# Attention scores on one core: two batches interleaved in 8 KB loads, all loads ahead of the stores, and head pairs in block-diagonal q weights

## Chip, cores and metric

The kernel runs on one core of a Trainium2 chip. The metric is the device time of one execution in microseconds (us), as the median of several runs.

## What is computed

For each of 8 batches and 8 heads, the scores of 512 queries against 512 keys of 64 elements, scaled by 1/8. Inputs and output are float32 in DRAM.

```python
batch, heads, seq, dim = 8, 8, 512, 64
# q, k: (batch, heads, seq, dim) float32
scale = 1.0 / np.sqrt(q.shape[-1])
return (np.einsum('bhqd,bhkd->bhqk', q, k) * scale).astype(np.float32)
```

The inputs are 16.8 MB together, the output is 67.1 MB.

## The kernel before

The kernel goes through the batches one by one. For each batch `load` (L56, L57) brings k and q in one transfer of 1 MB each into `kf` and `qf`. The eight heads are cut in two halves x of four heads g. A partition holds, for one head g and one stretch m of R = 16 adjacent sequence rows, the rows of both halves: two runs of 16 x 64 floats, 4 KB each. On the DRAM side the transfer is 128 entries of (g m) with two runs each, on the SBUF side 128 partitions.

The loads are issued on the queue of SyncE (SP), four batches ahead: those of batches 0 to 3 at the start, each further one after the first pair of stores of an earlier batch.

Each batch is cast to bf16 (L87) into `kb` and `qb`, where the two halves x stand side by side in 128 columns. GpSimd (POOL) does it for all batches but the first, which VectorE (DVE) and ScalarE (ACT) share. TensorE (PE) then transposes 128 x 128 blocks of k (L95) and q (L103) through an identity matrix into PSUM tiles `tp` of 128 x 1024. VectorE copies those of k into `kT` (L97), ScalarE those of q into `qT` (L105). After the transposes the 64 elements of half x = 0 are in partitions 0 to 63, those of x = 1 in 64 to 127.

The scores of a head need only 64 of the 128 rows of TensorE, so each matmul (L119) uses a quarter of the array: 64 rows (the half x) by 64 columns (64 queries, one of two heads h). Four such matmuls with 512 keys each fill one half w of two PSUM tiles `ps`:

```python
nc.tensor.matmul(out=pss[x][h * U:(h + 1) * U, w, :],
                 lhsT=qTh[rows, i + w, g, :], rhs=kTh[rows, g, :],
                 start=True, stop=True, tile_position=(x * D, h * U))
```

`evacuate` scales a `ps` tile (128 x 1024 floats) into the output tile `o`, in turn on ScalarE (L71) and VectorE (L73). An `o` tile is 2 MB: 128 partitions with 8 query rows of 512 scores each, 16 KB that lie together in DRAM. Each is stored in one transfer on SP's queue (L128), so there are 32 stores. There are six `o` buffers, and raw, bf16 and transposed buffers for 4, 2 and 2 batches.

A scheduler orders the instructions of each engine by the priorities of the program's order and by free buffers; each engine then executes its own list in order, and SP's list holds loads and stores together.

Of the kernel before, what the change touches and what calls it, by code (L numbers as in the profile page):

```python
# [1 line left out]

# [5 lines left out]


@with_exitstack  # L10
def kernel(
    ctx: ExitStack,
    tc: tile.TileContext,
    q: bass.AP,
    k: bass.AP,
    out: bass.AP,
):

    nc = tc.nc
    B, H, S, D = q.shape
    scale = 1.0 / (D ** 0.5)
    P = 128
    G = H // 2
    M = P // G
    R = S // M
    RO = 8  # L30
    HP = RO * P // S
    U = P // HP
    JJ = R // RO

    f32 = mybir.dt.float32
    bf16 = mybir.dt.bfloat16

    q_r = q.rearrange("b (x g) (m j) d -> b (g m) x (j d)", x=2, j=R)
    k_r = k.rearrange("b (x g) (m j) d -> b (g m) x (j d)", x=2, j=R)
    out_r = out.rearrange("b (x n h) (u i) k -> b x n (h u) i k", x=2, h=HP, i=RO)  # L40

    consts = ctx.enter_context(tc.tile_pool(name="consts", bufs=1))
    raw_pool = ctx.enter_context(tc.tile_pool(name="raw", bufs=4))
    bf_pool = ctx.enter_context(tc.tile_pool(name="bf", bufs=2))
    t_pool = ctx.enter_context(tc.tile_pool(name="t", bufs=2))
    out_pool = ctx.enter_context(tc.tile_pool(name="out", bufs=6))
    tpsum_pool = ctx.enter_context(tc.tile_pool(name="tpsum", bufs=2, space=bass.MemoryType.PSUM))
    psum_pool = ctx.enter_context(tc.tile_pool(name="psum", bufs=3, space=bass.MemoryType.PSUM))

    AHEAD = 4  # L50
    raws = {}

    def load(b):
        kf = raw_pool.tile([P, 2, R * D], f32, name="kf")
        qf = raw_pool.tile([P, 2, R * D], f32, name="qf")
        nc.sync.dma_start(out=kf, in_=k_r[b])  # L56
        nc.sync.dma_start(out=qf, in_=q_r[b])  # L57
        raws[b] = (qf, kf)

    load(0)  # L60
    identity = consts.tile([P, P], dtype=bf16)
    make_identity(nc, identity)
    for b in range(1, AHEAD):
        load(b)

    n_evac = 0

    def evacuate(dst, src):
        nonlocal n_evac
        if n_evac % 2 == 0:  # L70
            nc.scalar.mul(out=dst, in_=src, mul=scale)  # L71
        else:
            nc.vector.tensor_scalar(out=dst, in0=src, scalar1=scale, scalar2=None,  # L73
                                    op0=mybir.AluOpType.mult)
        n_evac += 1

    for b in range(B):
        qf, kf = raws.pop(b)
        kb = bf_pool.tile([P, R, 2, D], bf16, name="kb")
        qb = bf_pool.tile([P, R, 2, D], bf16, name="qb")  # L80
        for slab, dst in ((kf, kb), (qf, qb)):
            for x in range(2):
                if b > 0:
                    copy = nc.gpsimd.tensor_copy
                else:
                    copy = (nc.vector.tensor_copy, nc.scalar.copy)[x]
                copy(out=dst[:, :, x, :], in_=slab[:, x].rearrange("p (j d) -> p j d", j=R))  # L87


        kT = t_pool.tile([P, P, R], bf16, name="kT")  # L90
        qT = t_pool.tile([P, RO, P, JJ], bf16, name="qT")
        for j0 in range(0, R, 8):
            tp = tpsum_pool.tile([P, 8, P], bf16, name="tp")
            for j in range(8):
                nc.tensor.transpose(out=tp[:, j, :], identity=identity,  # L95
                                    in_=kb[:, j0 + j].rearrange("p x d -> p (x d)"))
            nc.vector.tensor_copy(out=kT[:, :, j0:j0 + 8], in_=tp.rearrange("d j p -> d p j"))  # L97
        IW = 8 // JJ
        for i0 in range(0, RO, IW):
            tp = tpsum_pool.tile([P, IW, JJ, P], bf16, name="tp")  # L100
            for i in range(IW):
                for jj in range(JJ):
                    nc.tensor.transpose(out=tp[:, i, jj, :], identity=identity,  # L103
                                        in_=qb[:, RO * jj + i0 + i].rearrange("p x d -> p (x d)"))
            nc.scalar.copy(out=qT[:, i0:i0 + IW], in_=tp.rearrange("d i jj p -> d i p jj"))  # L105

        kTh = kT.rearrange("d (g m) j -> d g (m j)", g=G)
        qTh = qT.rearrange("d i (g m) jj -> d i g (m jj)", g=G)
        for g0 in range(0, G, 2):
            os = [out_pool.tile([P, 2 // HP, RO, S], f32, name="o") for _ in range(2)]  # L110
            for n in range(2 // HP):
                for i in range(0, RO, 2):
                    pss = [psum_pool.tile([P, 2, S], f32, name="ps") for _ in range(2)]
                    for w in range(2):
                        for h in range(HP):
                            g = g0 + n * HP + h
                            for x in range(2):
                                rows = slice(x * D, (x + 1) * D)
                                nc.tensor.matmul(out=pss[x][h * U:(h + 1) * U, w, :],  # L119
                                                 lhsT=qTh[rows, i + w, g, :],  # L120
                                                 rhs=kTh[rows, g, :],
                                                 start=True, stop=True,
                                                 tile_position=(x * D, h * U))
                    for x in range(2):
                        evacuate(os[x][:, n, i:i + 2, :], pss[x])
            for x in range(2):
                n0 = g0 // HP
                nc.sync.dma_start(  # L128
                    out=out_r[b, x, n0:n0 + 2 // HP].rearrange("n p i k -> p n (i k)"),
                    in_=os[x].rearrange("p n i k -> p n (i k)"))  # L130
            if g0 == 0 and b + AHEAD < B:
                load(b + AHEAD)


# [1 line left out]
_INS = ['q', 'k']  # L136
_OUTS = [((8, 8, 512, 512), 'float32')]


# [23 lines left out]
```

## Time and profile before

| What | Value |
|---|---|
| Median of 9 runs | 205.96 us (205.76 to 206.25) |
| The profiled execution | 205.96 us, span 204.0 us |
| PE busy | 130.2 us (64% of the span) |
| DVE busy | 94.5 us (46%) |
| ACT busy | 82.9 us (41%) |
| POOL busy | 29.0 us (14%) |
| DMA | 84.01 MB, 8,969 packets, mean 412 GB/s |

The span goes from the first to the last instruction that the profile shows; the execution's own time has about 2 us around it. Busy times are sums over the span, and the engines run side by side. A DMA transfer is cut into packets that sixteen DMA engines move; its time to landing counts from its issue on SP's queue to the last of its bytes.

### The profile page before, as it was taken

What the parts mean: (1) busy time and instruction counts of PE and PEld (TensorE: products, weight loads), DVE (VectorE), ACT (ScalarE), POOL (GpSimd) and SP (SyncE); (2) the same over time, 40 slices, a digit from 0 to 9 for tenths busy, and PEclk for the clock granted to TensorE, in tenths of its full rate; (3) what the DMA queues carried; (4) which work ended last, traced back from release to release, by engine and by line L of the source; (5) the groups of instructions that cost most, each with busy time, mean ns of one, the idle gap of its engine ahead of it and who ended that gap; (6) DMA issues with size and microseconds to landing.
All of it is one profiled execution on the core that took longest, in us unless ns stands there. A gap on an engine that the chain in (4) does not pass through costs nothing.

```text
span 204.0 us, 1911 instructions
## 1 busy us (share of the span) xinstructions
PE 130.2 (64%) x768; PEld 45.0 (22%) x768; DVE 94.5 (46%) x82; ACT 82.9 (41%) x83; POOL 29.0 (14%) x34
## 2 busy tenths in 40 slices
PE   0398878775969659696486955969777677600000
PEld 0363423261103511034110421104211111000000
DVE  0549896912639036490546706366718081800000
ACT  2476978263522625227252453417552515200000
POOL 1077530510006100070000700000000000000000
PEclk9999999855555555558555585555555555555555
DMA  6999999999999999999999999999999999999991
GB/s 206 421 410 411 445 418 402 446 430 421 437 402 433 440 424 417 434 425 434 437 404 426 435 418 440 434 421 437 421 430 443 422 430 424 434 437 418 440 408 58
DMA packets 8969, 84.01 MB, mean 412 GB/s; under 512 B 768, under 2 KB 768, under 8 KB 4864
## 3 DMA queue, kind: packets, MB, share of 16 engines
q1 hardware_dynamic: 8960, 83.89, 97.6%
q8 instruction: 6, 0.10, 0.2%
q14 instruction: 3, 0.02, 0.0%
HBM read 16.78 MB, written 67.11 MB: 411 GB/s over the span
## 4 chain that ended last, share of the span: by engine, by line
DMA 60%; DVE 16%; PE 6%; ACT 4%; issue 1%; SPq 0%; DVEq 0%
DMA out_dram<-o 57%; DVE o L73 12%; PE ps L119 4%; DMA qf<-in_q_dram 3%; DVE kT L97 3%; ACT o L71 2%; ACT qT L105 1%; PE tp L103 1%; PE tp L95 1%; DVE qb L87 0%; SPq L56 0%; SPq L128 0%; DVEq L73 0%
## 5 line engine op out<-in xcount | busy, mean ns | idle before, releaser
L119 PE MATMUL ps<-kT,qT 64*64 64x512 bf16 x512 | 103.6, 559 | 37.5 <-ACT o L71 23.9
L73 DVE TENSOR_SCALAR o<-ps 128x1024 f32<-128x1024 f32 x64 | 75.2, 1219 | 76.3 <-DMA out_dram<-o 65.0
L71 ACT ACTIVATE o<-ps 128x1024 f32<-128x1024 f32 x64 | 64.5, 1025 | 77.1 <-PE ps L119 65.9
L119 PEld LDWEIGHTS <-qT 64*64 64x64 bf16 x512 | 22.5, 124 | 110.6 <-issue 107.9
L87 POOL CAST kb<-kf 128x1024 bf16<-128x1024 f32 x14 | 14.2, 1040 | 81.0 <-DMA kf<-in_k_dram 80.5
L105 ACT COPY qT<-tp 128x1024 bf16<-128x1024 bf16 x16 | 16.2, 1014 | 12.7 <-PE tp L103 12.4
L97 DVE COPY kT<-tp 128x1024 bf16<-128x1024 bf16 x16 | 18.9, 1216 | 0.6 <-PE tp L95 0.6
L95 PE MATMUL tp<-identity,kb 128*128 128x128 bf16 x128 | 13.2, 267 | 7.7 <-ACT kb L87 6.8
L103 PE MATMUL tp<-identity,qb 128*128 128x128 bf16 x128 | 15.1, 286 | 2.2 <-DVE kT L97 1.4
L87 POOL CAST qb<-qf 128x1024 bf16<-128x1024 f32 x14 | 14.2, 1040 | 6.1 <-DMA qf<-in_q_dram 4.2
L103 PEld LDWEIGHTS <-qb 128*128 128x128 bf16 x128 | 11.7, 131 | 9.6 <-issue 8.6
L95 PEld LDWEIGHTS <-kb 128*128 128x128 bf16 x128 | 11.0, 123 | 11.4 <-ACT kb L87 6.8
L87 DVE CAST kb<-kf 128x1024 bf16<-128x1024 f32 x1 | 0.7, 695 | 5.7 <-DMA kf<-in_k_dram 5.7
L87 ACT CAST kb<-kf 128x1024 bf16<-128x1024 f32 x1 | 1.0, 1045 | 3.6 <-DMA kf<-in_k_dram 3.6
L87 ACT CAST qb<-qf 128x1024 bf16<-128x1024 f32 x1 | 1.0, 1044 | 1.5 <-DMA qf<-in_q_dram 1.5
L87 ACT ACT_TABLE_LOAD x1 | 1.3, 1283 | 0.7 <-PEq L147 0.7
L87 DVE CAST qb<-qf 128x1024 bf16<-128x1024 f32 x1 | 0.7, 695 | 1.8 <-DMA qf<-in_q_dram 1.8
masks.py:199 POOL TENSOR_SCALAR_AFFINE_SELECT identity<-identity 128x128 bf16<-128x128 bf16 x1 | 0.3, 292 | 0.1
masks.py:197 POOL MEMSET identity<- 128x128 bf16 x1 | 0.2, 204 | 0.3 <-POOLq L147 0.3
L147 POOL MEMSET const-float32-0.0<- 128x1 f32 x1 | 0.1, 98 | 0.2 <-issue 0.2
L147 POOL MEMSET const-bfloat16-1.0<- 128x1 bf16 x1 | 0.1, 102 | 0.0
L147 POOL MEMSET const-uint8-127<- 128x1 uint8 x1 | 0.1, 102 | 0.0
(1 smaller groups left out, 0.1 us busy)
## 6 DMA issues: line engine op xcount, KB each, us to landing
out_dram<-o SPq DMA_DIRECT2D x32, 2048.0 KB, 25.0
kf<-in_k_dram SPq DMA_DIRECT2D x8, 1024.0 KB, 17.0
qf<-in_q_dram SPq DMA_DIRECT2D x8, 1024.0 KB, 19.5
```

The costliest lines, as they stand in the source:

```text
L71: nc.scalar.mul(out=dst, in_=src, mul=scale)
L73: nc.vector.tensor_scalar(out=dst, in0=src, scalar1=scale, scalar2=None, op0=mybir.AluOpType.mult)
L87: copy(out=dst[:, :, x, :], in_=slab[:, x].rearrange("p (j d) -> p j d", j=R))
L95: nc.tensor.transpose(out=tp[:, j, :], identity=identity, in_=kb[:, j0 + j].rearrange("p x d -> p (x d)"))
L97: nc.vector.tensor_copy(out=kT[:, :, j0:j0 + 8], in_=tp.rearrange("d j p -> d p j"))
L103: nc.tensor.transpose(out=tp[:, i, jj, :], identity=identity, in_=qb[:, RO * jj + i0 + i].rearrange("p x d -> p (x d)"))
L105: nc.scalar.copy(out=qT[:, i0:i0 + IW], in_=tp.rearrange("d i jj p -> d i p jj"))
L119: nc.tensor.matmul(out=pss[x][h * U:(h + 1) * U, w, :], lhsT=qTh[rows, i + w, g, :], rhs=kTh[rows, g, :], start=True, stop=True, tile_posi ...
L147: nc = _bacc.Bacc("TRN2", target_bir_lowering=False, num_devices=1)
```

## The change

There are two parts.

The first is another layout of the work. A unit is now two batches (v, with b = 0 or 1), so there are four units. A head number is n and x, with x the lower bit, so the two heads of a pair are adjacent. A transfer brings one x of one unit: 128 partitions of (m, b, n), m being a stretch of R = 32 sequence rows, 8 KB in one run. On the DRAM side this is 16 entries of m with 8 runs (b n) each; on the SBUF side it is 128 partitions. There are 16 loads of 1 MB as before. `load_and_cast` is called for all units before any scores, so that on SP's queue the 16 loads stand ahead of all 32 stores; four raw buffers, now of 8 KB for each partition, hold the loads in flight, and a load waits until the load four before it is cast. The casts, of 128 x 2048 elements each, go into five `xb` buffers. There are five `o` buffers instead of six.

The second is the use of TensorE. The transposed q of the two heads x of a pair goes into a tile `qz` whose other quarters are zero: rows of x = 0 have their 64 queries in columns 0 to 63, rows of x = 1 in columns 64 to 127. One matmul over the full array (128 rows, 128 columns, 512 keys) gives the scores of both heads; two such matmuls do what four in quarters did. Two `qz` tiles are cleared once at the start, one quarter by VectorE and three by GpSimd. The copies of transposed k are shared between VectorE and ScalarE, and a transposed q tile takes two copies of 64 partitions each, one on either engine.

In the changed kernel the loads are L70, the casts L75, the clears L82, the transposes L91 (k) and L100 (q), the copies L94 and L105, the matmul L116, the evacuations L57 and L59, the stores L120.

```diff
-    G = H // 2
-    M = P // G
+    UNITS = B // 2
+    C = H
+    M = P // C
     R = S // M
     RO = 8
-    HP = RO * P // S
-    U = P // HP
+    U = S // RO
     JJ = R // RO
...
-    q_r = q.rearrange("b (x g) (m j) d -> b (g m) x (j d)", x=2, j=R)
-    k_r = k.rearrange("b (x g) (m j) d -> b (g m) x (j d)", x=2, j=R)
-    out_r = out.rearrange("b (x n h) (u i) k -> b x n (h u) i k", x=2, h=HP, i=RO)
+    q_r = q.rearrange("(v b) (n x) (m j) d -> v x m (b n) (j d)", b=2, x=2, j=R)
+    k_r = k.rearrange("(v b) (n x) (m j) d -> v x m (b n) (j d)", b=2, x=2, j=R)
+    out_r = out.rearrange("(v b) (n x) (u i) k -> v (b n) (x u) (i k)", b=2, x=2, i=RO)
...
-    bf_pool = ctx.enter_context(tc.tile_pool(name="bf", bufs=2))
+    bf_pool = ctx.enter_context(tc.tile_pool(name="bf", bufs=5))
...
-    out_pool = ctx.enter_context(tc.tile_pool(name="out", bufs=6))
+    out_pool = ctx.enter_context(tc.tile_pool(name="out", bufs=5))
...
+    def load_and_cast(v):
+        both = []
+        for src in (k_r, q_r):
+            xb = bf_pool.tile([P, R, 2, D], bf16, name="xb")
             for x in range(2):
-                if b > 0:
+                xf = raw_pool.tile([P, R * D], f32, name="xf")
+                nc.sync.dma_start(out=xf, in_=src[v, x])
+                if v > 0:
                     copy = nc.gpsimd.tensor_copy
                 else:
                     copy = (nc.vector.tensor_copy, nc.scalar.copy)[x]
-                copy(out=dst[:, :, x, :], in_=slab[:, x].rearrange("p (j d) -> p j d", j=R))
+                copy(out=xb[:, :, x, :], in_=xf.rearrange("p (j d) -> p j d", j=R))
+            both.append(xb)
+        return both
+    def clear(engine, qz, x):
+        rows = slice(x * D, (x + 1) * D)
+        engine.memset(qz[rows, :, :, (1 - x) * U:(2 - x) * U], 0.0)
...
+            copy = (nc.vector.tensor_copy, nc.scalar.copy)[n % 2]
+            copy(out=kT[:, :, :, j0:j0 + 8].rearrange("d c m j -> d m c j"),
+                 in_=tp.rearrange("d j (m c) -> d m c j", c=C))
...
-            nc.scalar.copy(out=qT[:, i0:i0 + IW], in_=tp.rearrange("d i jj p -> d i p jj"))
+            for x in range(2):
+                rows = slice(x * D, (x + 1) * D)
+                copy = (nc.vector.tensor_copy, nc.scalar.copy)[x]
+                copy(out=qz[rows, i0:i0 + IW, :, x * U:(x + 1) * U]
+                     .rearrange("d i c (m jj) -> d i c m jj", jj=JJ),
+                     in_=tp[rows].rearrange("d i jj (m c) -> d i c m jj", c=C))
+        return kT, qz
...
+    def scores(v, c, kT, qz):
+        o = out_pool.tile([P, RO, S], f32, name="o")
+        for i in range(0, RO, 2):
+            ps = psum_pool.tile([P, 2, S], f32, name="ps")
+            for w in range(2):
+                nc.tensor.matmul(out=ps[:, w, :], lhsT=qz[:, i + w, c, :],
+                                 rhs=kT[:, c].rearrange("d m j -> d (m j)"),
+                                 start=True, stop=True)
+            evacuate(o[:, i:i + 2, :], ps)
+        nc.sync.dma_start(out=out_r[v, c], in_=o.rearrange("p i k -> p (i k)"))
+
+    cast = [load_and_cast(0)]
...
+    qzs = [consts.tile([P, RO, C, P], bf16, name=f"qz{n}") for n in range(2)]
+    clear(nc.vector, qzs[0], 0)
+    clear(nc.gpsimd, qzs[0], 1)
+    for x in range(2):
+        clear(nc.gpsimd, qzs[1], x)
+    for v in range(1, UNITS):
+        cast.append(load_and_cast(v))
+
+    ts = {0: transpose(0, *cast[0])}
+    for v in range(UNITS):
+        for c in range(C):
+            scores(v, c, *ts[v])
+            if c == C // 2 - 1 and v + 1 < UNITS:
+                ts[v + 1] = transpose(v + 1, *cast[v + 1])
```

More of the change, by code (lines that the diff above doesn't have):

```diff
@@ L26 @@
     P = 128
-    G = H // 2
-    M = P // G
+    UNITS = B // 2
+    C = H
+    M = P // C
     R = S // M
     RO = 8
-    HP = RO * P // S
-    U = P // HP
+    U = S // RO
     JJ = R // RO
+    IW = 8 // JJ
     f32 = mybir.dt.float32
     bf16 = mybir.dt.bfloat16
-    q_r = q.rearrange("b (x g) (m j) d -> b (g m) x (j d)", x=2, j=R)
-    k_r = k.rearrange("b (x g) (m j) d -> b (g m) x (j d)", x=2, j=R)
-    out_r = out.rearrange("b (x n h) (u i) k -> b x n (h u) i k", x=2, h=HP, i=RO)
+    q_r = q.rearrange("(v b) (n x) (m j) d -> v x m (b n) (j d)", b=2, x=2, j=R)
+    k_r = k.rearrange("(v b) (n x) (m j) d -> v x m (b n) (j d)", b=2, x=2, j=R)
+    out_r = out.rearrange("(v b) (n x) (u i) k -> v (b n) (x u) (i k)", b=2, x=2, i=RO)
     consts = ctx.enter_context(tc.tile_pool(name="consts", bufs=1))
     raw_pool = ctx.enter_context(tc.tile_pool(name="raw", bufs=4))
-    bf_pool = ctx.enter_context(tc.tile_pool(name="bf", bufs=2))
+    bf_pool = ctx.enter_context(tc.tile_pool(name="bf", bufs=5))
     t_pool = ctx.enter_context(tc.tile_pool(name="t", bufs=2))
-    out_pool = ctx.enter_context(tc.tile_pool(name="out", bufs=6))
+    out_pool = ctx.enter_context(tc.tile_pool(name="out", bufs=5))
     tpsum_pool = ctx.enter_context(tc.tile_pool(name="tpsum", bufs=2, space=bass.MemoryType.PSUM))
     psum_pool = ctx.enter_context(tc.tile_pool(name="psum", bufs=3, space=bass.MemoryType.PSUM))
[L50 to L64, printed above, removed]
     n_evac = 0
@@ L75, in evacuate @@
         n_evac += 1
[L77 to L81, printed above, removed]
+    def load_and_cast(v):
+        both = []
+        for src in (k_r, q_r):
+            xb = bf_pool.tile([P, R, 2, D], bf16, name="xb")
             for x in range(2):
-                if b > 0:
+                xf = raw_pool.tile([P, R * D], f32, name="xf")
+                nc.sync.dma_start(out=xf, in_=src[v, x])
+                if v > 0:
                     copy = nc.gpsimd.tensor_copy
@@ L86, with transpose @@
                     copy = (nc.vector.tensor_copy, nc.scalar.copy)[x]
[L87 to L92, printed above, removed]
+                copy(out=xb[:, :, x, :], in_=xf.rearrange("p (j d) -> p j d", j=R))
[4 more added lines that the diff above has]
+        engine.memset(qz[rows, :, :, (1 - x) * U:(2 - x) * U], 0.0)
+    def transpose(v, kb, qb):
+        kT = t_pool.tile([P, C, M, R], bf16, name="kT")
+        qz = qzs[v % 2]
+        for n, j0 in enumerate(range(0, R, 8)):
             tp = tpsum_pool.tile([P, 8, P], bf16, name="tp")
@@ L96 @@
                                     in_=kb[:, j0 + j].rearrange("p x d -> p (x d)"))
-            nc.vector.tensor_copy(out=kT[:, :, j0:j0 + 8], in_=tp.rearrange("d j p -> d p j"))
-        IW = 8 // JJ
+            copy = (nc.vector.tensor_copy, nc.scalar.copy)[n % 2]
+            copy(out=kT[:, :, :, j0:j0 + 8].rearrange("d c m j -> d m c j"),
+                 in_=tp.rearrange("d j (m c) -> d m c j", c=C))
         for i0 in range(0, RO, IW):
@@ L104 @@
                                         in_=qb[:, RO * jj + i0 + i].rearrange("p x d -> p (x d)"))
[L105 to L125, printed above, removed]
-            for x in range(2):
[L127 to L132, printed above, removed]
@@ new lines @@
+    cast = [load_and_cast(0)]
+    identity = consts.tile([P, P], dtype=bf16)
+    make_identity(nc, identity)
+    qzs = [consts.tile([P, RO, C, P], bf16, name=f"qz{n}") for n in range(2)]
[11 more added lines that the diff above has]
+                ts[v + 1] = transpose(v + 1, *cast[v + 1])
```

## The prediction

> **What bounds the kernel now.** I read the slices of the span first, then the DMA queues and the chain of waits.
>
> ```profile
> DMA  6999999999999999999999999999999999999991
> GB/s 206 421 410 411 445 418 402 446 430 421 437 402 433 440 424 417 434 425 434 437 404 426 435 418 440 434 421 437 421 430 443 422 430 424 434 437 418 440 408 58
> ...
> q1 hardware_dynamic: 8960, 83.89, 97.6%
> q8 instruction: 6, 0.10, 0.2%
> ...
> HBM read 16.78 MB, written 67.11 MB: 411 GB/s over the span
> ...
> DMA 60%; DVE 16%; PE 6%; ACT 4%; issue 1%; SPq 0%; DVEq 0%
> ```
>
> The DMA row is full from the second slice to the last, at 400 to 446 GB/s, and queue q1 alone fills 97.6% of sixteen engines' span. The chain puts 60% on DMA, and most of the rest lies in o tiles that wait for one. The kernel moves 84 MB and is bound by that. Two stretches tell loads and stores apart (columns: stretch, its length, busy us of PE, PEld, DVE, ACT and POOL, clock, DMA share, GB/s).
>
> ```profile
> 4.00:20.00 16.00, 11.06 (x99) 6.88 (x100) 9.77 (x10) 8.80 (x9) 7.52 (x8) 1.00 1.03 413
> ...
> 140.00:190.00 50.00, 28.80 (x133) 6.98 (x132) 20.01 (x18) 17.67 (x18) 0.00 (x0) 0.50 1.01 430
> 190.00:200.00 10.00, 0.00 (x0) 0.00 (x0) 0.00 (x0) 0.00 (x0) 0.00 (x0) 0.50 0.91 390
> ```
>
> From 4 to 20 us there are only loads (4,096-byte packets): 413 GB/s. From 140 to 190 only stores (16,384-byte packets): 430 GB/s. In the last stretch the mean share is 0.91: some DMA engines are done before others. Compute does no work after some 180 us (slices). What the rest costs is in the groups and the DMA issues.
>
> ```profile
> L119 PE MATMUL ps<-kT,qT 64*64 64x512 bf16 x512 | 103.6, 559 | 37.5 <-ACT o L71 23.9
> L73 DVE TENSOR_SCALAR o<-ps 128x1024 f32<-128x1024 f32 x64 | 75.2, 1219 | 76.3 <-DMA out_dram<-o 65.0
> L71 ACT ACTIVATE o<-ps 128x1024 f32<-128x1024 f32 x64 | 64.5, 1025 | 77.1 <-PE ps L119 65.9
> ...
> L87 POOL CAST kb<-kf 128x1024 bf16<-128x1024 f32 x14 | 14.2, 1040 | 81.0 <-DMA kf<-in_k_dram 80.5
> L105 ACT COPY qT<-tp 128x1024 bf16<-128x1024 bf16 x16 | 16.2, 1014 | 12.7 <-PE tp L103 12.4
> L97 DVE COPY kT<-tp 128x1024 bf16<-128x1024 bf16 x16 | 18.9, 1216 | 0.6 <-PE tp L95 0.6
> ...
> out_dram<-o SPq DMA_DIRECT2D x32, 2048.0 KB, 25.0
> kf<-in_k_dram SPq DMA_DIRECT2D x8, 1024.0 KB, 17.0
> ```
>
> An o tile (2 MB) takes 2 x 1219 ns on DVE beside 2 x 1025 ns on ACT, and its store 2.10 MB / 430 GB/s = 4.9 us. Stores land 25 us after issue, five stores deep: much queue, so small delays of compute are hidden.
>
> The trace's packet records size the bound. Nearly all 4,096-byte packets took 159 ns and 16,384-byte ones 611 ns, overlapping by 4 ns: 155 and 607. Per engine that is 256 x 0.155 = 39.7 us of loads and 256 x 0.607 = 155.4 us of stores. The first packet starts at 1.85 us and takes 0.9. The sum is 197.7; the fastest engine's last packet ends at 198.5, the slowest's at 202.8. So the slowest lags by 4.3 us: the sixteen landings of one DMA spread over 0.18 us for the first loads and 4.4 us for the last store. Queue q8 is part of that: six fetches of 16 KB, 0.93 to 1.1 us each, and a data packet beside most of them grows from 611 to about 1010 ns. Span and median differ by 205.96 - 204.0 = 1.96 us; the profiled execution took 205.96, the median itself.
>
> [...] every transfer before has 128 rows on both sides, and 159 ns for nearly every packet shows no sharing. [...] The six fetches come at every 230 to 260 PE instructions[...].
>
> **The change part by part.**
>
> *Load runs.* 256 packets of 4 KB per engine become 128 of 8 KB. By the line through the two sizes, one costs 155 + 4096 x 452/12288 = 306 ns; 128 are 39.2 us. Gain: 0.5 us.
>
> *Shape of the loads.* This decides. Before, the DRAM side was 128 entries of (g m). Now it is 16 entries of m, each with 8 rows (b n); the SBUF side is still 128 partitions. [...] The engines start together (first packets end within 0.16 us[...])[...]. The row distance in DRAM (256 KB, now and then 1 MB) I cost at nothing: the halves of before lay 512 KB apart and read at 159 ns. No row of before shows shared ports. Bounds: nothing, 39.2 us, if ports do not bind or engines drift apart[...]. I take 1.8[...]. Cost: 39.2 x 0.8 = 31.4 us, all on the path, because the stores that follow need every engine for 155.4 us whatever happens.
>
> *All loads ahead of the stores on SP.* Order is no cost to a full queue. Loads 5 to 16 wait for the cast of the load four earlier; behind them on SP stand all later loads and all 32 stores. Unshared, a load lands, its cast takes 2 x 1.04 us on POOL, issue to first packet 1.1 us (0.74 to 1.85): 3.2 us, while three loads in flight last 3 x 2.45 = 7.3 us. Cover: 4 us; with slower loads more. The first store, issued at 19 us before, comes after the cast of load 12, near 35 us unshared, before the loads end at 42: no gap. Its tile is long done, and five o buffers then hold 5 x 4.9 = 24 us of queue.
>
> *POOL.* 28 casts of 1.04 us become 12 of about 2.1 (25 us), plus three clears of 4,096 bf16. A 128-element clear took 204 ns, a one-element one 98, so about 3.4 us each, 12 us in all before load 5 lands at 15. Twice that would take the 4 us of cover.
>
> *DVE and ACT.* One clear on DVE, 2,048 words, at most 2.4 us by L73's pace, before the first load lands at 5.6. Copies: k 16, now shared by both engines; q becomes 32 half-height ones for 16. That is 16 more at 1.0 to 1.2 us, 10 us on DVE and 8 on ACT over the span. DVE 94.5 and ACT 82.9 of 204 leave room; a unit with transposes delays one tile by some 7 us against 20 us of queued stores. Cost 0; without this cover 7 us for each of two units.
>
> *PE.* 512 matmuls in quarters become 256 over the full array with half the weights zero. At half clock 32 old ones kept PE busy 7.5 us from 50 to 60; if two ran side by side one takes 0.47 us, eight per o tile 3.8 us; L119's mean gives 4.5. Both are under 4.9. Transposes stay 256. Cost 0. PE instructions fall from 1,536 to 1,024, so fetches from six to four: lag 4.3 x 4/6 = 2.9, gain 1.4 us.
>
> *One o buffer fewer* (5 of 16 KB for 6): covered above.
>
> Sum: 202.8 - 0.5 - 1.4 + 31.4 = 232.3 us for the last packet, + 1.3 to the span's end = 233.6, + 1.96 = 235.5 us.
>
> **Rivals.**
>
> *A, faster: ports are not shared.* [...]engines drift out of step at once. For it: the 0.2 to 1 us stalls in packet records do shift engines, and nothing in the profile shows sharing. [...] Time: 205.96 - 0.5 - 1.4 = 204.1 us. It decides if the load factor is under 1.05 (39.2 x 0.05 = 2 us).
>
> *B, the load pipeline starves instead.* POOL's clears or casts run long, SP holds the stores. At 3.0 us per cast, 12 x 0.55 = 6.6 us less 4 us of cover: 204.1 + 2.6 = 206.7 us. Against: POOL's casts in before hold 1040 ns beside busy DVE.
>
> *C, it does not do what it says:* longer runs and fewer fetches bring nothing at the end, because other stalls set the slowest engine: 205.9 us.
>
> **How the numbers follow.** A measurement of this kernel can tell 0.2% from no change. Port sharing 0.74, A 0.20, B 0.04, C 0.02. The likeliest gives 235.5; its own range, factors 1.3 to 1.94, is 215.9 to 240.9. Because A holds 0.20, the range reaches down to it: 203.5 to 241. Slower: 0.74 + B's 0.03 = 0.77. Same: C's 0.02 and 0.01 of B. Faster: 0.20.
>
> **What would show it.** Right: the slices over the first 65 to 75 us at 220 to 260 GB/s with the DMA row still near 9, 8 KB packets of 500 to 600 ns, then 430 GB/s in stores; POOL waiting for loads; four fetches on q8; landings of a load spread over several us. Wrong: 415 GB/s or more over the first 42 us, 8 KB packets near 310 ns. A gap in the DMA row near 40 us would mean B, and stores waiting for o tiles in the middle that compute is the bound, which I exclude.

## The result, and the profile after

The changed kernel takes 239.75 us (median of 9 runs, 239.09 to 240.48), the kernel before 206.07 us in the runs beside it. The ratio is 1.1637, with a 95% interval from 1.1625 to 1.1649. The profiled execution has a span of 237.3 us.

The page of the changed kernel: slices of DMA share and of GB/s, the DMA queues, the bytes, and the chain of waits by engine.

```profile
DMA  6999999999999999999999999999999999999993
GB/s 156 220 232 218 226 221 221 221 221 222 224 224 221 427 428 425 434 431 431 423 435 431 435 417 434 431 439 420 431 434 439 424 425 431 439 431 425 428 439 144
...
q1 hardware_dynamic: 6912, 83.89, 98.3%
q8 instruction: 4, 0.07, 0.1%
...
HBM read 16.78 MB, written 67.11 MB: 353 GB/s over the span
...
DMA 63%; DVE 8%; PE 7%; ACT 6%; issue 3%; POOL 2%; SPq 1%; ACTq 0%; POOLq 0%
```

The DMA row is as full as before, 9 in every slice but the first and the last. The GB/s row below it is not: from the second slice to 77 us it stands at 218 to 232 GB/s, then it jumps to some 430. Queue q1 is busy for 98.3% of the span, more than before, to move the same bytes. This is how slow packets look: the engines are never idle and yet move half as much. DMA is the largest part of the chain, as before. Instruction fetches, on q8, are four instead of six.

Two stretches of the changed kernel (columns: stretch, its length, busy us of PE, PEld, DVE, ACT and POOL, clock, DMA share, GB/s).

```profile
4.00:76.00 72.00, 27.66 (x190) 17.26 (x191) 28.61 (x24) 25.49 (x24) 28.29 (x15) 0.85 1.02 223
90.00:200.00 110.00, 66.82 (x292) 27.77 (x292) 67.58 (x58) 55.20 (x57) 0.00 (x0) 0.84 1.01 430
```

Loads alone run at 223 GB/s, where they ran at 413 before; stores alone at 430, as before. By the packet records the first load packet starts at 2.2 us and the last one ends at 78.6: 76.4 us, against 39.2 by the prediction's price of 306 ns for an 8 KB packet, a factor of 1.95. The 76.4 us hold the slow first packets and the lag of the slowest engine too; packet against packet the factor is 1.87, since an 8,192-byte packet took 592 ns on average and 317 in the run with 128 rows below. The packets are not even: chains of one engine's packets repeat 618, 616, 525, 605 ns, a turn of four rows. One engine moves 4 x 8,192 bytes in that turn of 2,364 ns: 13.9 bytes per ns, about half of the 25.8 that 8,192 bytes in 317 ns make. Why the turn has four packets, no trace shows.

Groups and DMA issues of the changed kernel.

```profile
L116 PE MATMUL ps<-kT,qz 128*128 128x512 bf16 x256 | 86.2, 473 | 72.8 <-ACT o L57 67.6
L59 DVE TENSOR_SCALAR o<-ps 128x1024 f32<-128x1024 f32 x64 | 78.2, 1222 | 82.9 <-DMA out_dram<-o 60.1
L57 ACT ACTIVATE o<-ps 128x1024 f32<-128x1024 f32 x64 | 62.4, 1022 | 94.4 <-DMA out_dram<-o 82.3
...
L75 POOL CAST xb<-xf 128x2048 bf16<-128x2048 f32 x12 | 22.7, 1893 | 45.6 <-DMA xf<-in_k_dram 25.1
...
L105 DVE COPY qz<-tp 64x1024 bf16<-64x1024 bf16 x16 | 19.1, 1210 | 4.9 <-PE tp L100 4.9
...
L82 POOL MEMSET qz<- 64x4096 bf16 x3 | 11.5, 3830 | 0.1
...
out_dram<-o SPq DMA_DIRECT2D x32, 2048.0 KB, 21.2
xf<-in_k_dram SPq DMA_DIRECT2D x8, 1024.0 KB, 16.9
```

The evacuations cost what they did: L59 and L57 take 1222 and 1022 ns. The 256 matmuls on the full array keep PE busy for 86.2 us, the 512 in quarters took 103.6. (256 x 473 ns would be 121 us: the 473 ns of one count the time in which two overlap.) Compute waits for the loads at first and then for the stores; two of the longest waits (us in total, how many, the longest):

```profile
ACT o L57 <- DMA out_dram<-o: 82.3, 20, 26.4
...
POOL xb L75 <- DMA xf<-in_k_dram: 25.1, 5, 14.1
```

ACT's longest single wait, 26 us, is for a free o buffer: five tiles are ready by 58 us, and the first store is not moved before 77 us.

### The profile page after: what moved, and what is told of

It reads as the page before. It is cut to its first block, busy times and chain, and to the rows that moved or that the text cites. A ratio compares the mean times of both kernels' runs of the same rounds, so it can differ in the third digit from the quotient of the medians.

```text
span 237.3 us, 1462 instructions
## 1 busy us (share of the span) xinstructions
PE 106.1 (45%) x512; PEld 48.8 (21%) x512; DVE 109.6 (46%) x91; ACT 90.8 (38%) x91; POOL 34.9 (15%) x21
## 3 DMA queue, kind: packets, MB, share of 16 engines
q1 hardware_dynamic: 6912, 83.89, 98.3%
## 4 chain that ended last, share of the span: by engine, by line
DMA 63%; DVE 8%; PE 7%; ACT 6%; issue 3%; POOL 2%; SPq 1%; ACTq 0%; POOLq 0%
DMA out_dram<-o 47%; DMA xf<-in_q_dram 16%; PE ps L116 5%; DVE o L59 5%; ACT o L57 4%; POOL xb L75 2%; DVE qz L105 2%; ACT qz L105 1%; SPq L70 1%; PE tp L100 1%; DVE kT L94 1%; ACT xb L75 1%; SPq L120 0%; PE tp L91 0%; ACTq L57 0%
## 5 line engine op out<-in xcount | busy, mean ns | idle before, releaser
L116 PE MATMUL ps<-kT,qz 128*128 128x512 bf16 x256 | 86.2, 473 | 72.8 <-ACT o L57 67.6
L59 DVE TENSOR_SCALAR o<-ps 128x1024 f32<-128x1024 f32 x64 | 78.2, 1222 | 82.9 <-DMA out_dram<-o 60.1
L57 ACT ACTIVATE o<-ps 128x1024 f32<-128x1024 f32 x64 | 62.4, 1022 | 94.4 <-DMA out_dram<-o 82.3
L116 PEld LDWEIGHTS <-qz 128*128 128x128 bf16 x256 | 28.6, 115 | 121.6 <-issue 109.0
L75 POOL CAST xb<-xf 128x2048 bf16<-128x2048 f32 x12 | 22.7, 1893 | 45.6 <-DMA xf<-in_k_dram 25.1
L91 PE MATMUL tp<-identity,xb 128*128 128x128 bf16 x128 | 13.1, 260 | 22.0 <-ACT xb L75 14.7
L105 DVE COPY qz<-tp 64x1024 bf16<-64x1024 bf16 x16 | 19.1, 1210 | 4.9 <-PE tp L100 4.9
L105 ACT COPY qz<-tp 64x1024 bf16<-64x1024 bf16 x16 | 16.0, 1007 | 5.7 <-DVE qz L105 5.0
L100 PE MATMUL tp<-identity,xb 128*128 128x128 bf16 x128 | 11.8, 247 | 12.9 <-ACT qz L105 5.5
L91 PEld LDWEIGHTS <-xb 128*128 128x128 bf16 x128 | 11.0, 121 | 25.8 <-ACT xb L75 14.7
L100 PEld LDWEIGHTS <-xb 128*128 128x128 bf16 x128 | 10.0, 112 | 17.3 <-issue 9.4
L82 POOL MEMSET qz<- 64x4096 bf16 x3 | 11.5, 3830 | 0.1
L94 DVE COPY kT<-tp 128x1024 bf16<-128x1024 bf16 x8 | 9.8, 1220 | 3.6 <-PE tp L91 3.6
L94 ACT COPY kT<-tp 128x1024 bf16<-128x1024 bf16 x8 | 8.1, 1013 | 7.3 <-PE tp L91 7.3
L75 ACT CAST xb<-xf 128x2048 bf16<-128x2048 f32 x2 | 3.8, 1897 | 15.2 <-DMA xf<-in_k_dram 10.7
L75 DVE CAST xb<-xf 128x2048 bf16<-128x2048 f32 x2 | 2.6, 1324 | 13.0 <-DMA xf<-in_q_dram 8.0
L82 DVE MEMSET qz<- 64x2048 uint32 x1 | 1.8, 1765 | 1.2 <-PEq L153 1.2
```

Of the source, the lines that this page charges most:

```text
L75: copy(out=xb[:, :, x, :], in_=xf.rearrange("p (j d) -> p j d", j=R))
L82: engine.memset(qz[rows, :, :, (1 - x) * U:(2 - x) * U], 0.0)
L91: nc.tensor.transpose(out=tp[:, j, :], identity=identity, in_=kb[:, j0 + j].rearrange("p x d -> p (x d)"))
L94: copy(out=kT[:, :, :, j0:j0 + 8].rearrange("d c m j -> d m c j"), in_=tp.rearrange("d j (m c) -> d m c j", c=C))
L105: copy(out=qz[rows, i0:i0 + IW, :, x * U:(x + 1) * U] .rearrange("d i c (m jj) -> d i c m jj", jj=JJ), in_=tp[rows].rearrange("d i jj (m c ...
L116: nc.tensor.matmul(out=ps[:, w, :], lhsT=qz[:, i + w, c, :], rhs=kT[:, c].rearrange("d m j -> d (m j)"), start=True, stop=True)
```

## Experiments

The texts on record speak of ports that DMA engines share. No trace shows such a port, how many there are, or which partitions belong to one; that was the author's assumption. The runs show which loads and writes slow each other, and by how much.

**Undo the shape of the loads alone.** Same runs, sizes, buffers, order and compute; only the DRAM side of a load becomes 128 adjacent rows.

```diff
-    k_r = k.rearrange("(v b) (n x) (m j) d -> v x m (b n) (j d)", b=2, x=2, j=R)
+    k_r = k.rearrange("b h (m j) d -> (b h m) (j d)", j=R).rearrange("(v x p) e -> v x p e", x=2, p=P)
```

(q_r in the same way.)

> The changed kernel, except that the DRAM side of a load is 128 adjacent rows of 8 KB instead of 16 entries of 8 rows; runs, sizes, buffers, order on SP and all compute stay. The loads bring other rows into the partitions, so the scores come out for other rows. Theory[...] load factor 1.0, loads over by 42 us, 415 to 425 GB/s in the load stretch, 8 KB packets near 310 ns, time 204.1 us (203 to 205). Rival 1 (8 KB runs are slow in themselves) and rival 2 (loads alone, without stores beside them, or four raw buffers, are slow): no change, 237 to 241 us.

Measured: 203.85 us, ratio to before 0.9898 (0.9882 to 0.9915). Its page:

```profile
DMA  6999999999999999999999999999999999999992
GB/s 221 427 414 425 428 414 423 425 428 431 428 435 435 425 431 428 425 436 428 430 435 428 425 435 425 435 428 435 431 426 431 428 431 431 428 431 431 435 428 110
...
q8 instruction: 4, 0.07, 0.1%
```

From the second slice on the row is at 414 GB/s or more; 8 KB packets took 309 ns at the median, and the loads are over at 44.5 us. So 8 KB runs, loads without stores beside them and four raw buffers cost nothing: rivals 1 and 2 fall. The shape of the DRAM side is worth 239.75 - 203.85 = 35.9 us, the whole loss and more.

**Where the rows lie in DRAM.** Two runs separate the number of entries from their distance. In the first, 128 entries stay but lie 64 KB apart (`"(p v x) e -> v x p e"` in the line above). In the second there are 16 entries of 8 rows, and the 8 rows are adjacent:

```diff
+    def near(src, v, x):
+        t0 = (2 * v + x) * 125
+        return src[t0:t0 + 144].rearrange("(m r) e -> m r e", r=9)[:, 0:8]
...
-                nc.sync.dma_start(out=xf, in_=src[v, x])
+                nc.sync.dma_start(out=xf, in_=near(src, v, x))
```

> As the run with 128 adjacent rows, but the 128 rows of a load lie 64 KB apart in DRAM. The loads bring other rows, so the scores come out for other rows. Theory of shared ports: where the rows lie in DRAM doesn't matter, only that there are 128 entries: 203 to 206 us, packets near 310 ns. Rival 3 (rows far apart in DRAM are slow, in the changed kernel 256 KB and 1 MB): clearly slower than with adjacent rows, 220 us or more.

> The changed kernel with 16 entries of 8 rows kept, but the 8 rows of an entry adjacent in DRAM (64 KB in one piece) and the entries 72 KB apart. The loads bring other rows, so the scores come out for other rows. Theory of shared ports: still 237 to 241 us, packets of 520 to 630 ns[...]. Rival 3 (row distance in DRAM): fast, 204 to 210 us.

Measured: 203.72 us with 128 rows far apart (ratio 0.9894, 0.9879 to 0.9909), 237.65 us with 16 entries of adjacent rows (a single run). The load stretch of each, columns as above, far rows first:

```profile
4.00:40.00 36.00, 22.02 (x162) 14.27 (x163) 29.55 (x22) 23.36 (x22) 26.57 (x14) 1.00 1.01 424
```

```profile
4.00:76.00 72.00, 26.76 (x190) 16.80 (x191) 31.56 (x24) 25.42 (x24) 28.46 (x15) 0.85 1.01 228
```

424 against 228 GB/s: the far rows are fast and the near rows slow. Rival 3 falls. Of the two it is the number of entries on the DRAM side that matters.

**The shape alone, put into the kernel before.** Its loads get 16 entries of 8 rows by another order of rows; runs stay at 4 KB, loads stay between stores. Since each load had to be cut in two, a control cuts them in two with 128 rows.

```diff
-    k_r = k.rearrange("b (x g) (m j) d -> b (g m) x (j d)", x=2, j=R)
+    k_r = k.rearrange("b (x g) (t r j) d -> b r (g t) x (j d)", x=2, r=16, j=R)
...
-        nc.sync.dma_start(out=kf, in_=k_r[b])
-        nc.sync.dma_start(out=qf, in_=q_r[b])
+        for dst, src in ((kf, k_r), (qf, q_r)):
+            for x in range(2):
+                nc.sync.dma_start(out=dst[:, x], in_=src[b][:, :, x])
```

(The control has the last four lines, with `src[b][:, x]`, and the old pattern.)

> The kernel before, with the rows of a load put into the partitions in another order, so that its DRAM side is 16 entries of 8 rows of 4 KB (each load cut in two by the half x, since the pattern has no room for it; the copies out of the transposes undo the order). Theory of shared ports: 4 KB packets of up to 300 ns instead of 159 while engines are in step. In step throughout, the cost is 39.7 x 0.94 = 37 us, 243 us; but here loads stand between stores, and the landings of a DMA spread over 1.5 us and more after the first 28 us[...], so I expect the later loads to be hit less: 220 to 243 us. Rivals 1 and 2 (8 KB runs, all loads first): 205 to 207 us.

> The kernel before with each load cut in two by the half x, 512 KB each with 128 rows of 4 KB on the DRAM side: the control for the run of the kernel before with 16 entries. Theory: 205.9 to 207 us, since[...] only 16 more issues on SP are added. If the cut were what cost the time there: 225 us or more.

Measured, a single run each: 231.16 us with 16 entries, 207.77 us for the control. Their GB/s rows, 16 entries first:

```profile
GB/s 159 234 231 233 235 229 308 429 309 288 420 446 420 297 318 435 426 432 284 384 426 435 408 322 424 437 426 429 429 432 435 426 432 426 432 432 429 437 420 106
```

```profile
GB/s 233 388 418 410 432 443 392 416 446 417 446 396 435 436 420 423 422 439 423 430 409 409 436 428 430 436 420 436 420 439 420 443 423 436 420 443 423 433 315 38
```

With 16 entries the second to the sixth slice, loads alone, run at 229 to 235 GB/s, and later dips to about 300 stand where loads lie between stores. So the shape slows 4 KB runs too: 231.16 - 207.77 = 23.4 us. That is less than the 37 us forecast for engines in step throughout. The 4 KB packets took 285 ns on average up to the first store packet at 37.7 us and 241 ns after it, against 164 and 165 in the control, so the later loads are hit less, as expected. That this comes of stores which spread the engines apart is not shown. The control is 0.8 us over its expected range: the landings of its last store spread over 6.2 us against 4.4 before, and why that engine is later was not traced.

**Is it being in step?** If engines slow each other because they write at the same time, an offset between them should free them. The first attempt adds two small transfers behind the first load, of 12 rows and of 4, meant to hold some engines longer than others:

```diff
+    scratch = consts.tile([40, 1920], f32, name="scratch")
+    rows = k.rearrange("b h (m j) d -> (b h m) (j d)", j=R)
+    def offset():
+        nc.sync.dma_start(out=scratch[0:12, 0:1920], in_=rows[0:12, 0:1920])
+        nc.sync.dma_start(out=scratch[36:40, 0:1920], in_=rows[16:20, 0:1920])
```

> The changed kernel with two small extra transfers behind the first load on SP's queue: 12 rows of 7.5 KB[...] into partitions 0 to 11, then 4 rows[...] into partitions 36 to 39, into a scratch tile that nothing reads. [...] Theory of shared ports in step: more bytes[...]; first load at half rate, the others at 1.06 to 1.15 of full time: loads over by 45 to 50 us instead of 78, time 207 to 213 us. If the offset is lost soon (sharing that is not even, or fast engines that run out of issued loads), 215 to 235. Rival: the 16-entry split is slow for a reason other than two engines at one port at a time (descriptors, DRAM): 240 to 244 us.

Measured: 238.84 us (ratio 1.1575, 1.1524 to 1.1626), so no gain. Three stretches of it, columns as above:

```profile
4.00:7.00 3.00, 0.00 (x0) 0.00 (x0) 0.00 (x0) 0.00 (x0) 2.92 (x3) 1.00 1.00 222
7.40:9.20 1.80, 0.00 (x0) 0.00 (x0) 0.36 (x1) 0.00 (x0) 1.75 (x2) 1.00 0.97 118
12.00:76.00 64.00, 29.11 (x190) 17.70 (x191) 28.08 (x24) 25.43 (x24) 19.69 (x11) 0.86 1.01 228
```

The extra transfers do not make the offset. Right after them the rate falls to 118 GB/s: packets of all sixteen engines took 900 to 1,225 ns, though the extra transfers write only partitions 0 to 11 and 36 to 39, and by 9.5 us all are in step again. How so few writes hold up all engines is not shown. The run with each transfer twice was the control for this one:

> As the run with the two extra transfers, but each of them twice (to other partitions)[...]. Theory of shared ports in step: load factor 1.8 to 1.95 again, 236 to 245 us. If the extra transfers as such, and not the offset that they make, were what helps: 207 to 215 us.

It took 238.49 us (a single run), within its range, but since the single offset had failed it tells nothing more.

The second attempt makes the offset without SBUF, by copies from DRAM to DRAM.

```diff
+    rows = k.rearrange("b h (m j) d -> (b h m) (j d)", j=4 * R)
+    scratch = nc.dram_tensor("scratch_dram", (16, 8192), f32, kind="Internal").ap()
+    def offset():
+        nc.sync.dma_start(out=scratch[0:12, 0:8000], in_=rows[0:12, 0:8000])
+        nc.sync.dma_start(out=scratch[12:16, 0:8000], in_=rows[12:16, 0:8000])
```

> The offset tried again without writing to SBUF: behind the first load, 12 rows of 32,000 bytes are copied from DRAM to a DRAM scratch[...], then 4 rows[...], which nothing reads. Each holds its engines for about 1.2 us[...]. If sharing is bound to the engines being in step and offsets last: packets near 310 to 350 ns after some 8 us, loads over by 45 to 50 us, 207 to 213 us. If something pulls the engines back into step[...]: packets of 520 to 630 ns again within a few us, 237 to 243 us.

Measured: 210.62 us (a single run). DMA share and GB/s by slices, and the stretch from 12 to 44 us:

```profile
DMA  5999999999999999999999999999999999999992
GB/s 127 332 386 397 397 386 391 366 375 435 430 424 439 417 439 433 424 433 419 438 439 421 433 424 436 436 424 436 425 436 424 433 430 430 433 424 439 433 421 119
```

```profile
12.00:44.00 32.00, 23.06 (x172) 14.90 (x173) 24.47 (x22) 23.44 (x22) 16.41 (x10) 1.00 1.02 386
```

The same 16-entry loads, with half a megabyte of useless copies added, now run at 386 GB/s. Nine packets in ten take 309 to 373 ns from 8 to 36 us, and up to 430 ns from there to the end of the loads at 51.2 us. The copies took 1.19 to 1.44 us each, and only some engines take part in each transfer: the page counts 784 packets under 512 B where the 128-row run has 768, sixteen for each of 48 loads and stores, so the two extra transfers have sixteen together. Nothing about a load was changed but when some engines start it, so what halves the rate is that the engines go through a load in step, and an offset of this kind, once made, lasted until the loads ended.

One engine by itself does not get free so. In the changed kernel a fetch on q8 takes one engine from 40.0 to 41.2 us. The sixteen landings of one load, within 0.47 us before that, then spread over 1.8 to 1.9 us for eight loads: fifteen stay close together and one comes 1.3 to 1.5 us after them, so this engine stays behind. Yet no load packet from 4 to 75 us took less than 515 ns: the lag brought neither this engine nor any other near the 309 ns of the offset above. Why is open.

**Partitions far apart or close together.** In the 8 KB kernel below, small transfers, each of 11 or 16 DRAM entries of one row each, write (a) 11 partitions that lie 12 apart, (b) 16 that lie 4 apart, (c) 16 adjacent ones. In the first form, shown here, with packets of 3,840, 3,712 and 3,584 bytes, the three parts ran into each other; in the second, with 1,920, 1,856 and 1,792 bytes, a 128-row load stands between them.

```diff
+    for n, (count, step, width) in enumerate(((11, 12, 960), (16, 4, 928), (16, 1, 896))):
+        scratch = consts.tile([P, 2, 960], f32, name=f"scratch{n}")
+        for r in range(4):
+            first = (r, r, 16 * r)[n]
+            nc.sync.dma_start(out=scratch[first:first + step * (count - 1) + 1:step, :, 0:width],
+                              in_=rows[64 * n + 16 * r:64 * n + 16 * r + count]
+                              .rearrange("p (c w) -> p c w", c=2)[:, :, 0:width])
```

> The kernel with 8 KB loads of 128 rows and quarter matmuls, plus twelve small transfers behind its first four loads, into scratch tiles that nothing reads. All twelve have one DRAM entry of two packets for each engine, as the 16-entry loads have one of eight, so they differ in nothing but which partitions are written[...]. Theory of shared ports[...]: steady packets of about (a) 146 ns, (b) 273 ns, (c) 527 ns[...]. Rival (the split by entries is slow by itself): all three alike per byte, near 280 ns. Nothing of interest lies in the total time, 206 to 213 us.

Packets of (a) took 149 ns until shortly after the first of (b) began, then, from 12.75 us on, 230 to 306 ns without exception, though five of the eleven partitions in each of its transfers lie above 63, where (b) writes nothing; (b) took 142 to 440 ns, (c) 140 to 474. As a price list this form is inconclusive; it shows writes slowing each other again, in partitions well apart too.

> The port test again with a 128-row load between its three parts, so that parts don't run into each other; two transfers of four packets for each engine per part[...]. All have one DRAM entry for each engine, and what is written goes to scratch tiles that nothing reads. Theory of shared ports[...]: most packets about (a) 76 ns, (b) 141 ns, (c) 268 ns[...]. Rival (the split by entries is slow by itself): all near 140 ns. The total time is of no interest, 206 to 212 us.

With the parts apart (two transfers of four packets each in a part, widths 480, 464 and 448), (a) took 79 ns for nearly all packets; (b) took 76 ns for its first ones and then mostly 125 to 160; (c) began at 74 and settled at 180 to 280. (a) and (b) are near what was expected; (c) stays under the expected 268 ns in most packets; why is not shown. All three parts have few entries on the DRAM side, and (a) moves 1,920 bytes in 79 ns, 24.3 bytes per ns, near the 25.8 of a packet in the 128-row loads: few entries are not slow by themselves. Packets of nearly the same size took 1.6 to 2 times as long with sixteen partitions 4 apart, and mostly 2.3 to 3.5 times with sixteen adjacent ones; between these two only the distance of the partitions differs. The two runs took 212.72 and 209.96 us in total, the second inside its range and the first at the top of its own.

**8 KB runs with 128 entries and quarter matmuls.** x becomes the batch of a unit, so that a load is one batch in one piece; this gives up the block-diagonal weights, because the two heads of a pair are no longer adjacent in the output, and takes the quarter matmuls and the plain q tile of before.

```diff
-    k_r = k.rearrange("(v b) (n x) (m j) d -> v x m (b n) (j d)", b=2, x=2, j=R)
-    out_r = out.rearrange("(v b) (n x) (u i) k -> v (b n) (x u) (i k)", b=2, x=2, i=RO)
+    k_r = k.rearrange("(v x) h (m j) d -> v x (h m) (j d)", x=2, j=R)
+    out_r = out.rearrange("(v x) (n h) (u i) k -> v x n (h u) (i k)", x=2, h=2, i=RO)
```

> 8 KB loads and all loads first kept, but with 128 entries on the DRAM side: x is the batch of a unit instead of the head's parity, so a load is one batch of q or k in one piece of 1 MB, and the scores use the quarter matmuls and the plain q tile of the kernel before (1,536 PE instructions, no clears). Theory: loads at full rate; against the kernel before only the 0.5 us of longer runs is gained, since fetches stay six: 205.4 us (204.6 to 206). Rival: the block-diagonal half of the change brings nothing, and this is as fast as the changed kernel with 128-row loads: 203.8 us.

Measured: 204.70 us (204.54 to 204.91), ratio to before 0.9936 (0.9923 to 0.9950). GB/s by slices and fetches:

```profile
GB/s 223 423 432 418 421 423 418 423 421 429 442 423 429 436 423 423 439 429 426 436 429 421 442 421 432 432 426 432 432 423 436 428 426 439 426 423 439 423 420 61
...
q8 instruction: 6, 0.10, 0.2%
```

This beats both kernels, by 0.6% over before (the runs with 128 rows above, faster still, bring other rows). With the fetches still six it is 0.85 us slower than the changed kernel with 128-row loads, whose fetches are four; the two differ in matmuls, copies and clears as well, so the 0.85 us belong to that half of the change as a whole.

## Why the prediction was right

*The bound, and the step that decided.* The forecast was 235.5 us in a range up to 241, slower, by engines that slow each other in the loads; measured 239.75, 1.25 us inside the end of that range. That the shape of the loads halves their rate, and that engines in step slow each other, is shown by four things together: the load rate of 223 GB/s with 16 entries; 422 and 424 GB/s with 128 entries, adjacent or 64 KB apart; the test of partitions, where 11 entries alone cost nothing (79 ns) and 16 partitions close together did (mostly 125 to 280 ns); and the offset, which brings 386 GB/s and 210.62 us. That it is ports is not shown, nor which partitions an engine gets in a 16-entry load: no record names engine and partition, and both were the author's assumption.

*The term that was mis-sized.* It is "I take 1.8" for the load factor. The rest of the forecast, 204.1 us, came to 203.85 in the run with 128 rows, so the shape cost 35.9 us instead of 31.4: 39.2 x 0.92, a factor of 1.92. That is 4.5 us too little for the shape, less 0.25 too much for the rest: the miss of 4.25 us. The 1.8 was the author's estimate; nothing in the profile before could size it. All engines ran at the same rate, about half of what they had with 128 rows: 223 GB/s in all against 422. The landings of one load spread over 0.45 us in the first seven loads and 1.1 to 1.9 us in the others, not over "several us".

*The small gains.* The runs with 128 rows give them without the loads' loss. Rival A's 204.1 us is met by 203.85. The first landing of the last store moves from 198.81 to 198.11 us (longer runs: 0.7, forecast 0.5), and the spread of its landings from 4.41 to 3.14 us (forecast 2.9 from 4.3), each in one profiled execution. Not all of that need be the fetches: the kernel with six fetches and 8 KB loads has 4.02, so four for six are worth at most 0.9 us rather than 1.4. In the run with 128 rows only the first of the four fetches, at 29.6 us, comes with a jump of the spread, from 0.74 to 1.69 us. That the number of fetches sets the end is so not shown.

*Costed at nothing, rightly.* Order on SP: in the run with 128 rows no slice shows a gap at 42 us. POOL: 1.9 us for a cast (2.1 forecast), 3.8 for a clear (3.4). The matmuls kept PE busy for 86.2 / 256 = 0.34 us each, where 0.47 was forecast for half clock; the clock granted was 0.80 over the span, not half. Compute ends at 215 us, with stores queued to the end, so the copies added to DVE and ACT and the o buffer that was dropped stay hidden. The distance of rows in DRAM costs nothing: 203.72 against 203.85 us.

*Rivals.* A did not decide, but it is what remains when the shape is undone. B's gap and C's unchanged time did not come.

## What to carry to other kernels

Read GB/s beside DMA share: here a share of 9 in the load slices at 223 GB/s went with packets of 592 ns, where the run with 128 rows had 317 ns and 422 GB/s: the packets themselves were slow. The cause was in the transfer's shape, not in its order or buffers. Before a load is rearranged for longer runs, count the entries of its outermost dimension on both sides: here 128 to 128 ran at 422 GB/s, and 16 to 128 cost 36 us of 204. Runs of 8 KB instead of 4 KB were worth 0.7 us, so a layout that gives up the 128 rows for them lost.

## What the hardware showed that was not expected

A few small writes to partitions close together slowed all engines: 118 GB/s in all for 1.8 us in the first attempt at an offset. In the test of partitions, where parts (a) and (b) ran into each other, the packets of (a) grew from 149 to over 230 ns, without exception, though (b) writes no partition above 63 and (a) does.

And engines in step stayed in step. An offset of 1.2 to 1.4 us, made once near 8 us by copies of 12 rows and then 4, kept most packets at 309 to 430 ns for 43 us and through 15 loads. Without it all sixteen engines ran at half rate for 76 us, and one engine put 1.3 us behind the others at 40 us did not change that, for itself or for any other.
